# Overflow branch moved behind expert 13, the turn of expert 1 one unit later, the last projection piece reordered

## The chip, the cores and the metric

The kernel runs on one core of a Trainium2 chip. Its time is the device time of one execution in microseconds (us). A core has TensorE (PE, with PEld for its weight loads), VectorE (DVE), ScalarE (ACT), GpSimd (POOL) and SyncE (SP), each with its own queue of instructions that it works off in order, and 16 DMA engines that move data between the chip's memory and the core's.

## The reference

An encoder of two layers on 512 tokens of 1024 numbers, all in fp32. Each layer is an attention part and a mixture of experts:

```python
h = rms_norm(x, norm1_g[layer])
proj = jnp.einsum('bsd,dc->bsc', h, w_in[layer])          # cut into the inputs of four mixers
y_a = mla_mixer(...); y_b = dilated_mixer(...); y_c = gqa_mixer(...); y_d = diff_mixer(...)
mixed = jnp.concatenate([rms_norm(y_a), rms_norm(y_b), rms_norm(y_c), y_d], axis=-1) * mix_beta[layer]
x = x + jnp.einsum('bsm,md->bsd', mixed, w_out[layer])
x = x + hier_moe(rms_norm(x, norm2_g[layer]), ...)
# hier_moe: router picks one of 4 groups, then 2 of its 4 experts for each token; then
for e in range(N_EXPERTS):                                # 16
    hid = jax.nn.silu(t @ w_gate[e]) * (t @ w_up[e])      # 1024 -> 512
    y = y + gate[:, e:e + 1] * (hid @ w_down[e])          # 512 -> 1024
```

## The kernel before

**Products.** Weights come as fp32. ACT rounds a block of 128x1024 to `hi` (L155), DVE, in some places POOL, computes the rest `lo` (L156), and PE makes each product in three passes, hi by xh, lo by xh, hi by xl (`mm3`, L299). Expert 0 alone is multiplied in plain fp32 (L1504).

**Weights.** The class `Weights` (L158) holds all weights of the program in one list, in the order of their use, as units of 512 KB. SP issues their loads in that order, each as soon as a raw buffer comes free; a raw buffer comes free when its unit is split. Six pairs of hi and lo may be ahead of their use. In the expert stretch there are some 29 raw buffers, a few of them parts of the tile `x_sb` that the stretch does not need.

**Order.** The program is written under a manual schedule: each engine's instructions stand in its queue in the order in which the Python code issues them.

**Projection.** `stage` (L667) makes one piece of the in-projection for the four tiles of 128 tokens: `proj` issues the products of a tile, `W.split` the split of one more weight unit, `F.pump` some steps of a filler (here the norm of a mixer's queries and keys: a square on ACT, L451, and its sum on DVE, L455), and `ev()` the evacuation of the product by ACT (L763). The piece that begins at column 2208 is the last. Behind it come 64 attention units, each with a maximum over the scores on DVE (L936) and the exponent on ACT (L955); weights of the out-projection are split in between.

**Experts.** Each expert takes the tokens that chose it, up to 96, by a list. POOL gathers them from memory (`gather`), PE transposes them (`turn`, L1492), ACT and DVE split the transposed tokens into `xh` and `xl`. The matrices follow each other as `MOE_ORDER` says: (0, g), (0, u), (1, g), (0, d), (1, u), (2, g), (1, d), (2, u), ... (14, g), (13, d), (14, u), (15, g), (14, d), (15, u), (15, d), where g is gate, u up and d down, each of four units. After g comes the SiLU on ACT (`silu`, L1511), after d the weighting on ACT (`store`, L1546) and a scatter-add into memory by POOL.

**Overflow.** If an expert has more than 96 tokens, `overflow` (L1550) runs further rounds over all experts. It is a branch (L1562) on a number that every engine reads from the chip's memory; with these inputs the number is 1 and nothing of the body runs. The queues go through the branch one by one: what stands behind it on an engine is issued when that engine has passed it. In the kernel before it stands behind the store of expert 0, with the SiLU of expert 1 after it.

Of the kernel before, what the change touches and what calls it, by code (L numbers as in the profile page):

```python
# [21 lines left out]
NT = 4  # L22
EPS = 1e-6
NE = 16
# [39 lines left out]
def hybrid_encoder(ctx: ExitStack, tc: tile.TileContext, I: dict, out: bass.AP, depth=2, dbg=None):  # L64
# [183 lines left out]
    W = Weights()  # L248
# [105 lines left out]
    for layer in range(depth):  # L354
# [6 lines left out]
        X = {}  # L361
# [25 lines left out]
        with ExitStack() as c2:  # L387
# [203 lines left out]
            with ExitStack() as c3:  # L591
# [37 lines left out]
                def turned(t):  # L629
                    for k in range(0, 8, 4):  # L630
                        pt = turn([hs[t][:, (k + j) * 128:(k + j + 1) * 128] for j in range(4)])
                        split(hTh[t][:, k:k + 4], hTl[t][:, k:k + 4], pt.rearrange("p (a b) -> p a b", b=128))
# [21 lines left out]
                def proj(c0, t, evac, mid=None):  # L654
                    us, per, n = wbase[layer, 'in', c0]
                    pm = ps.tile([128, 512], FT, name="pm", tag="mm")[:, :n]
                    for i, u in enumerate(us):
                        wh, wl = W.get(u)
                        if mid and i == 2:
                            mid()  # L660
                        mm3(pm, [(hTh[t][:, k], hTl[t][:, k]) for k in range(i * per, (i + 1) * per)],
                            [(wh[:, j], wl[:, j]) for j in range(per)], first=i == 0, last=i == len(us) - 1)
                    if t == NT - 1:
                        W.free(us[-1] + 1)
                    return lambda: evac(t, pm)

                def stage(c0, evac, budget, then={}):  # L667

                    us = wbase[layer, 'in', c0][0]
                    for t in range(NT):  # L670
                        ev = proj(c0, t, evac)
                        for _ in side:
                            break
                        W.split(W.done + 1)
                        F.pump(budget)
                        if t == NT - 1:
                            W.split(us[-1] + 1 + 4)
                        ev()
                        if t in then:
                            then[t]()  # L680

# [79 lines left out]
                def copy_to(dst):  # L761
                    def ev(t, pm):
                        A.activation(dst[:, t], pm, AF.Copy, scale=rs[t])  # L763
                    return ev
# [15 lines left out]
                if layer == 0:  # L780
# [6 lines left out]
                    ev = proj(0, 1, ev_a, lambda: turned(2))  # L787
# [6 lines left out]
                    ev = proj(0, 2, ev_a, lambda: turned(3))  # L794
# [4 lines left out]
                for t in range(NT if layer else 0):  # L799
# [12 lines left out]
                    if t == 1:  # L812
                        ev = proj(0, 0, ev_a)
# [4 lines left out]
                    if t == 2:  # L818
                        ev = proj(0, 1, ev_a)
                        turned(2)  # L820
                    if t == 3:
# [4 lines left out]
                        ev = proj(0, 2, ev_a)  # L826
# [4 lines left out]
                ev = proj(0, 3, ev_a)  # L831
# [20 lines left out]
                od = O[3] = outputs(3, 256, 32, "pc", ap_)  # L852
# [1 line left out]
                assert lat['normed']  # L854
                stage(1696, copy_to(od[0]), 4, {0: lambda: prepare(heads[0], 0), 1: lambda: prepare(heads[0], 1)})
                F.add(norm(od, gains['diff_qk_g'], 32))
                stage(2208, copy_to(od[3]), 1)
                for _ in side:
                    pass
                del TP['hp']  # L860
# [2 lines left out]
            with ExitStack() as c3:  # L863
# [431 lines left out]
                g, d = list(range(32, 48)), list(range(48, 56))  # L1295
# [6 lines left out]
                for k, hd in enumerate(heads):  # L1302
                    first, m = place[k * NT], len(hd[2])
# [79 lines left out]
        with ExitStack() as c2:  # L1383
# [221 lines left out]
            def start(e):  # L1605
# [3 lines left out]
                else:  # L1609
# [5 lines left out]
                          m=lambda: G.memset(xg[1], 0.0), S=lambda: start(1), K=weights,  # L1615
                          q=lambda: G.tensor_copy(parts[..., :2], tokb[:, :, None].to_broadcast([128, NT, NE, 2])))
            tail(TAIL[len(seq) + 5])
            for e, m in MOE_ORDER:
                us = wbase[layer, e, m][0]
                for i, u in enumerate(us):  # L1620
                    W.split(u + 1)
                    end = e == NE - 1 and m != 'g'
                    if m == 'd':
                        X[e].down(i, W.get(u))
                    elif end:
                        X[e].half(i, W.get(u))
                    else:
                        X[e].gu(m, i, W.get(u))
                    W.free(u + 1)
                    if end:  # L1630
                        if m == 'u' and i % 2:
                            X[e].hidden(i // 2)
                        if (m, i) == ('u', 2) or (m, i) == ('d', 0):
                            X[e].turn_hidden(m == 'd')
                    elif m == 'g' and i == 0 and e > 0:
                        X[e - 1].hidden()
                    upto = moe_units[-1] + 1
                    if end and m == 'd' and i > 1:
                        upto += W.RAW
                    W.split(min(u + (AHEAD if end else W.HL), upto), G if (m, i) in GS and not end else V)  # L1640
                    if m == 'g' and i == TH and e > 0:
                        X[e - 1].turn_hidden()
                    if m == 'u' and i == 1 and e + 1 < NE:
                        X[e + 1].turn()

                    for s, todo in FIRST if e < 2 else ((e + 3, (('u', 0), ('u', 2))),):
                        if e > 1:
                            todo = [(e,) + w for w in todo]
                        if (e, m, i) in todo and s < NE:
                            (start if (e, m, i) == todo[1] else listed)(s)  # L1650
                    if m == 'd' and e < 2:
                        if i == 0:
                            X[e].hots = hots(e, sm.tile([128, NT, CAP], BF, name="oh", bufs=2))
                        elif i == 2:
                            X[e].lists(lambda t: parts[:, t, e], rows=e == 0)
                    if m == 'g' and i == 0 and e == NE - 1 and not last:
                        (place, g1), = W.room(1)
                        g1 = g1.bitcast(FT)
                        SP.dma_start(g1, _bcast(I['norm1_g'][layer + 1]))
                    if m == 'u' and i == 0 and e == NE - 1 and not last:  # L1660

                        pt = ps.tile([128, NT, 128], FT, name="pto", tag="tr")
                        for t in range(NT):
                            PE.matmul(pt[:CAP, t], X[e].hots[t], identb, start=True, stop=True)
                        place = place[:, :512].rearrange("p (t c) -> p t c", t=NT)
                        A.activation(place[:CAP], pt[:CAP], AF.Copy)
                        V.tensor_copy(wlast, gate[:, :, NE - 1])
                if m == 'g' and e != 1:
                    X[e].silu()
                elif m == 'd' and (last or e < NE - 1):  # L1670
                    X[e].store()
                if (e, m) == (0, 'd'):

                    overflow()
                    X[1].silu()
                if m == 'd' and e == NE - 2 and not last:

                    for t in range(NT):
                        SP.dma_start(x_sb[:, t], stream[:, t])
# [91 lines left out]
```

## Time and profile before

| | us |
|---|---|
| median of three runs | 1387.91 (1387.12 to 1390.14) |
| the profiled execution | 1392.77 |
| its span | 1391.0 |
| PE busy | 1290.2 (93% of the span) |
| DVE busy | 1057.1 (76%) |
| ACT busy | 857.8 (62%) |
| POOL busy | 359.9 (26%) |

The mean granted clock of TensorE over the span is 0.971. The program moves 278.44 MB, 200 GB/s on average. The two expert stretches are those in which the page's DMA row stands at nine tenths: roughly from 380 to 670 us and from 1060 to 1350 us. An idle time of an engine stands in brackets behind the instruction that ended it, with the engine or the transfer that released it.

### The profile page before, as it was taken

To read this page: it belongs to the slowest core of one execution; us is meant where nothing else is said; L and a number is where in the kernel's file an instruction comes from. 1 tells how busy PE (TensorE), PEld (TensorE's weight loads), DVE (VectorE), ACT (ScalarE), POOL (GpSimd) and SP (SyncE) were. 2 spreads that over 40 slices of the span, in tenths; PEclk is the share of its full clock that TensorE was granted. 3 is DMA by queue.
4 is the path that set the end of the run, shared out by engine and by line. 5 is a ranking of instruction groups with operands and counts; after the bars stand their busy time and mean duration, and the time that the engine had idled before them with its cause. 6 is when DMAs were issued, how large, how long until landed. Compare 5 with 4: busy or idle time off the path is not lost. (4 is left out here: it accounts for less than half of the span.)

```text
span 1391.0 us, 21081 instructions
## 1 busy us (share of the span) xinstructions
PE 1290.2 (93%) x7182; PEld 1003.5 (72%) x7182; DVE 1057.1 (76%) x2073; ACT 857.8 (62%) x1419; POOL 359.9 (26%) x580
## 2 busy tenths in 40 slices
PE   9998899999986999999989998999998699999996
PEld 7776688888844666666778886888885366676674
DVE  5537866878575999999776587586966499999994
ACT  5343366664245888888744545676634378888884
POOL 3105333324411411111041161430344132111120
PEclk9999899999998999999999999999999899999998
DMA  8322341024597999999344223211176899999950
GB/s 230 100 78 63 133 138 41 15 67 168 217 382 264 352 366 362 366 365 329 109 118 125 78 75 79 69 37 31 48 307 239 303 312 358 370 365 366 367 201 13
DMA packets 100575, 278.44 MB, mean 200 GB/s; under 512 B 19466, under 2 KB 30522, under 8 KB 100457
## 3 DMA queue, kind: packets, MB, share of 16 engines
q1 hardware_dynamic: 89816, 249.00, 49.9%
q0 software_dynamic: 10352, 27.41, 7.9%
q8 instruction: 58, 0.95, 0.3%
q10 hardware_dynamic: 288, 0.59, 0.1%
q14 instruction: 61, 0.49, 0.1%
HBM read 264.34 MB, written 24.81 MB: 208 GB/s over the span
## 5 line engine op out<-in xcount | busy, mean ns | idle before, releaser
L156 DVE TENSOR_TENSOR lo<-raw,hi 128x1024 fp32r<-128x1024 f32 (+2 forms) x387 | 463.9, 1221 | 64.2 <-ACT hi L155 56.1
L155 ACT ACTIVATE hi<-raw 128x1024 fp32r<-128x1024 f32 (+1 forms) x393 | 405.4, 1051 | 99.6 <-PE pg L299 28.7
L299 PE MATMUL pm<-lo,hTh 128*128 128x512 f32 (+2 forms) x376 | 132.5, 352 | 5.9 <-DVE lo L156 5.9
L299 PE MATMUL pm<-hi,hTh 128*128 128x512 f32 (+2 forms) x376 | 134.3, 357 | 0.7 <-ACT hTh L155 0.5
L299 PE MATMUL pm<-hi,hTl 128*128 128x512 f32 (+2 forms) x376 | 132.0, 351 | 0.2
L299 PE MATMUL pd<-hi,hl 128*96 128x512 f32 x256 | 102.5, 400 | 4.5 <-DVE hl L156 2.8
L986 PE MATMUL pv<-v,pT 128*128 128x64 f32 x768 | 99.0, 272 | 6.5 <-DVE pT L974 2.7
L299 PE MATMUL pd<-lo,hh 128*96 128x512 f32 x256 | 101.2, 395 | 1.6 <-DVE lo L156 1.6
L986 PEld LDWEIGHTS pv<-v,pT 128*128 128x128 f32 x768 | 94.3, 193 | 10.8 <-DVE pT L974 5.0
L299 PE MATMUL pu<-hi,xh 128*96 128x512 f32 (+1 forms) x256 | 101.1, 395 | 0.6 <-PEq L1562 0.6
L299 PE MATMUL pd<-hi,hh 128*96 128x512 f32 x256 | 101.2, 395 | 0.0
L957 ACT ACTIVATE p<-p,m 128x512 f32<-128x512 f32 x96 | 68.7, 716 | 52.1 <-DVE m L939 51.7
L299 PE MATMUL pu<-hi,xl 128*96 128x512 f32 (+1 forms) x256 | 98.2, 384 | 0.0
L299 PE MATMUL pu<-lo,xh 128*96 128x512 f32 (+1 forms) x256 | 98.2, 384 | 0.0
L299 PE MATMUL pg<-hi,xh 128*96 128x512 f32 x240 | 96.8, 404 | 0.0
L299 PE MATMUL pg<-lo,xh 128*96 128x512 f32 x240 | 95.6, 398 | 0.0
L299 PE MATMUL pg<-hi,xl 128*96 128x512 f32 x240 | 95.3, 397 | 0.0
L299 PEld LDWEIGHTS pm<-lo,hTh 128*128 128x128 f32 x376 | 71.0, 189 | 16.0 <-DVE lo L156 8.0
L299 PEld LDWEIGHTS pm<-hi,hTh 128*128 128x128 f32 x376 | 70.9, 188 | 12.0 <-ACT hTh L155 1.0
L299 PEld LDWEIGHTS pm<-hi,hTl 128*128 128x128 f32 x376 | 71.0, 189 | 9.5 <-DVE hTl L156 0.9
L307 PE MATMUL ptr<-ident,p 128*128 128x128 f32 x512 | 77.3, 273 | 0.3 <-DVE pT L974 0.2
L307 PEld LDWEIGHTS ptr<-ident,p 128*128 128x128 f32 x512 | 63.8, 141 | 17.7 <-DVE pT L974 1.2
(389 smaller groups left out, 2772.5 us busy)
## 6 DMA issues: line engine op xcount, KB each, us to landing
raw<-in_expert_w_down_dram SPq DMA_DIRECT2D x118, 512.0 KB
raw<-in_expert_w_gate_dram SPq DMA_DIRECT2D x114, 512.0 KB
raw<-in_expert_w_up_dram SPq DMA_DIRECT2D x110, 512.0 KB
raw<-in_w_in_dram SPq DMA_DIRECT2D x32, 512.0 KB
raw<-in_w_out_dram SPq DMA_DIRECT2D x16, 512.0 KB
toep<-brep SPq DMA_DIRECT2D x16, 448.0 KB
x_sb<-in_expert_w_gate_dram SPq DMA_DIRECT2D x14, 512.0 KB
x_sb<-in_expert_w_up_dram SPq DMA_DIRECT2D x10, 512.0 KB
```

What stands on the lines that cost most here:

```text
L155: A.activation(hi, src, AF.Copy)
L156: E.tensor_tensor(lo, src, hi.bitcast(FT), op=OP.subtract)
L299: PE.matmul(pt, a, b, start=first and n == 0, stop=last and n == tot - 1)
L307: PE.transpose(pt[:c, i * 128:(i + 1) * 128], s, ident)
L957: A.activation(p, p, AF.Exp, bias=m, scale=-1.0, accum_out=s)
L986: PE.matmul(st['pv'][:, t], self.pT[:, k * 128:(k + 1) * 128], self.v(k), start=k == 0, stop=k == NT - 1)
```

## The change

Three edits. `stage` gets a flag for the last piece: there the evacuation comes first, then, for the first two tiles only, one split, then the filler, and the splits of up to four units at the end are left out. The turn of expert 1 stands after the third unit of expert 0's up matrix and no longer after the second. The overflow branch stands behind expert 13's store, and the SiLU that comes after it is expert 14's.

```diff
-                def stage(c0, evac, budget, then={}):
+                def stage(c0, evac, budget, then={}, final=False):
                     us = wbase[layer, 'in', c0][0]
                     for t in range(NT):
                         ev = proj(c0, t, evac)
                         for _ in side:
                             break
-                        W.split(W.done + 1)
+                        if final:
+                            ev()
+                        if not final or t < 2:
+                            W.split(W.done + 1)
                         F.pump(budget)
-                        if t == NT - 1:
-                            W.split(us[-1] + 1 + 4)
-                        ev()
+                        if not final:
+                            if t == NT - 1:
+                                W.split(us[-1] + 1 + 4)
+                            ev()
...
-                stage(2208, copy_to(od[3]), 1)
+                stage(2208, copy_to(od[3]), 1, final=True)
...
-                    if m == 'u' and i == 1 and e + 1 < NE:
+                    if m == 'u' and i == (1 if e else 2) and e + 1 < NE:
                         X[e + 1].turn()
...
-                if m == 'g' and e != 1:
+                if m == 'g' and e != NE - 2:
                     X[e].silu()
                 elif m == 'd' and (last or e < NE - 1):
                     X[e].store()
-                if (e, m) == (0, 'd'):
+                if (e, m) == (NE - 3, 'd'):
                     overflow()
-                    X[1].silu()
+                    X[NE - 2].silu()
```

In the changed kernel the lines behind `stage` stand five further down (the branch is L1567 there, the SiLU L1516, the store L1551, the turn L1497, the evacuation L768).

ACT's queue in layer 0, at the old place of the branch, before. `ye` is the store of expert 0, `sg` the SiLU of expert 1, `xh` the tokens of expert 2; the branch's body is left out:

```order
L155 ACTIVATE hi<-x_sb 128x1024
L1546 ACTIVATE ye<-pd,w 96x512 x2
L1553 TENSOR_LOAD nrd
L1562 COMPARE_AND_BRANCH
...
L1562 UNCONDITIONAL_BRANCH
L1511 ACTIVATE sg<-pg 96x512
L155 ACTIVATE hi<-x_sb 128x1024
L155 ACTIVATE hi<-raw 128x1024
L155 ACTIVATE xh<-ptg 128x384 x2
```

The same place in the changed kernel:

```order
L155 ACTIVATE hi<-raw 128x1024
L1516 ACTIVATE sg<-pg 96x512
L155 ACTIVATE hi<-raw 128x1024 x3
L155 ACTIVATE hi<-x_sb 128x1024
L1551 ACTIVATE ye<-pd,w 96x512 x2
L155 ACTIVATE hi<-x_sb 128x1024
L155 ACTIVATE hi<-raw 128x1024
L155 ACTIVATE xh<-ptg 128x384 x2
```

The SiLU of expert 1 has moved up to the end of its gate, and between the store and the next splits nothing stands any more. The new place in the changed kernel, ACT's queue behind the store of expert 13, where `sg` is the SiLU of expert 14 and `xh` the tokens of expert 15:

```order
L155 ACTIVATE hi<-raw 128x1024 x5
L1551 ACTIVATE ye<-pd,w 96x512 x2
L1558 TENSOR_LOAD nrd
L1567 COMPARE_AND_BRANCH
...
L1567 UNCONDITIONAL_BRANCH
L1516 ACTIVATE sg<-pg 96x512
L155 ACTIVATE hi<-raw 128x1024 x2
L155 ACTIVATE xh<-ptg 128x384 x2
L155 ACTIVATE hi<-raw 128x1024 x5
```

Here two splits and the tokens of the last expert stand behind the branch. On SP all loads of a layer's expert weights now stand ahead of the branch, where before all but those of the first experts stood behind it.

PE's queue at the turn of expert 1 in layer 0, before (`pu` is expert 0's up product, `pli` the list of expert 0):

```order
L1504 MATMUL pu<-raw,xh 96x512 x4
L1492 MATMUL ptg<-ident,xg 128x96 x8
L1504 MATMUL pu<-raw,xh 96x512 x4
L1465 LDWEIGHTS oh
L1465 MATMUL pli<-parts,oh 96x5
```

And now:

```order
L1509 MATMUL pu<-raw,xh 96x512 x6
L1497 MATMUL ptg<-ident,xg 128x96 x8
L1509 MATMUL pu<-raw,xh 96x512 x2
L1470 LDWEIGHTS oh
L1470 MATMUL pli<-parts,oh 96x5
```

Two products, one unit, have moved ahead of the transposes. ACT's queue in the last projection piece of layer 0, before, up to the first attention unit's exponent (`h` is the filler's square, `v` the evacuation):

```order
L451 ACTIVATE h<-qk_1151 128x512
L763 ACTIVATE v_1152<-pm,r0y 128x256
L155 ACTIVATE hi<-raw 128x1024
L451 ACTIVATE h<-qk_1151 128x512
L763 ACTIVATE v_1152<-pm,r1y 128x256
L451 ACTIVATE h<-qk_1151 128x512
L763 ACTIVATE v_1152<-pm,r1y 128x256
L155 ACTIVATE hi<-raw 128x1024
L451 ACTIVATE h<-qk_1151 128x512
L763 ACTIVATE v_1152<-pm,r1y 128x256
L955 ACTIVATE p,den<-sc,m 128x512
```

And now:

```order
L768 ACTIVATE v_1152<-pm,r0y 128x256
L155 ACTIVATE hi<-raw 128x1024
L451 ACTIVATE h<-qk_1151 128x512
L768 ACTIVATE v_1152<-pm,r1y 128x256
L155 ACTIVATE hi<-raw 128x1024
L451 ACTIVATE h<-qk_1151 128x512
L768 ACTIVATE v_1152<-pm,r1y 128x256
L451 ACTIVATE h<-qk_1151 128x512
L768 ACTIVATE v_1152<-pm,r1y 128x256
L451 ACTIVATE h<-qk_1151 128x512
L960 ACTIVATE p,den<-sc,m 128x512
```

Each evacuation has moved ahead of a square, and between the third square and the exponent no split stands any more. The split that is missing here stands among the attention units, with its lo half on POOL.

## Rows read from the trace of the kernel before

**Rows 1.** Windows: start:end, length, busy PE, PEld, DVE, ACT, POOL, clock, DMA share, GB/s

```profile
446.00:660.00 214.00, 211.87 (x1031) 148.12 (x1030) 198.59 (x266) 176.48 (x211) 42.46 (x23) 1.00 1.01 358
660.00:664.00 4.00, 4.00 (x22) 2.87 (x21) 3.36 (x5) 3.35 (x6) 0.00 (x0) 1.00 0.44 181
1342.00:1346.00 4.00, 4.00 (x19) 2.81 (x18) 3.37 (x4) 3.85 (x5) 0.00 (x0) 1.00 0.18 75
424.00:446.00 22.00, 13.41 (x55) 9.47 (x56) 14.30 (x25) 13.04 (x16) 1.28 (x1) 0.77 0.63 203
1100.00:1124.00 24.00, 12.02 (x45) 8.02 (x44) 11.46 (x19) 10.00 (x13) 1.25 (x1) 0.72 0.62 194
```

**Rows 2.** Timeline, PE behind the branch: start, length, instruction, idle before and releaser

```profile
416.25 0.45 PE L299 MATMUL pu<-hi,xh 128*96 128x512 f32 x1 [0.30 <-PEq L1562]
...
432.59 0.78 PE L1465 MATMUL pli<-parts,oh 128*96 128x5 bf16 x4 [11.30 <-DVE oh L372]
...
1112.74 0.78 PE L1465 MATMUL pli<-parts,oh 128*96 128x5 bf16 x4 [11.98 <-DVE oh L372]
```

**Rows 3.** Timeline, ACT's first instruction behind the branch, layer 0

```profile
429.56 0.59 ACT L1511 ACTIVATE sg<-pg 96x512 f32<-96x512 f32 x1 [12.19 <-SPq L1562]
```

**Rows 4.** Timeline, SP's loads across the branch, layer 0

```profile
417.19 15.54 SPq L195 DMA_DIRECT2D x_sb<-in_expert_w_down_dram  x2
```

**Rows 5.** Windows behind the branch's stall, layers 0 and 1

```profile
432.00:438.00 6.00, 5.41 (x18) 3.79 (x19) 5.96 (x14) 3.87 (x7) 0.70 (x1) 0.60 0.63 181
1112.00:1120.00 8.00, 7.25 (x21) 4.94 (x22) 7.65 (x16) 4.96 (x7) 1.25 (x1) 0.54 0.68 202
```

**Rows 6.** Timeline, PE at the turn of expert 1, both layers

```profile
388.95 3.60 PE L1504 MATMUL pu<-raw,xh 128*96 128x512 f32 x8
396.49 1.51 PE L1492 MATMUL ptg<-ident,xg 96*128 96x96 f32 x8 [3.94 <-DMA xg<-h2d,nrd]
...
1076.24 1.51 PE L1492 MATMUL ptg<-ident,xg 96*128 96x96 f32 x8 [4.58 <-DMA xg<-h2d,nrd]
```

**Rows 7.** Windows behind the turn, layers 0 and 1

```profile
396.00:404.00 8.00, 7.51 (x21) 3.69 (x22) 1.85 (x7) 0.98 (x2) 0.00 (x0) 0.59 1.03 419
1076.00:1084.00 8.00, 7.76 (x23) 3.95 (x24) 2.31 (x10) 0.98 (x2) 0.00 (x0) 0.63 1.03 418
```

**Rows 8.** Timeline, ACT at the end of the last projection piece, layer 0

```profile
156.18 0.63 ACT L451 ACTIVATE h<-qk 128x512 f32<-128x512 f32 x1 [9.56 <-DVE ssq L455]
...
158.26 1.06 ACT L155 ACTIVATE hi<-raw 128x1024 fp32r<-128x1024 f32 x1 [1.09 <-DMA raw<-in_w_out_dram]
...
159.75 0.46 ACT L763 ACTIVATE v<-pm,r1y 128x256 f32<-128x256 f32 x1
```

**Rows 9.** Timeline, PE at the same place

```profile
157.23 1.09 PE L307 MATMUL ptr<-ident,qm 128*96 128x128 f32 x4 [5.68 <-ACT v L763]
```

**Rows 10.** Timeline, ACT, the store of expert 13, both layers

```profile
667.19 1.24 ACT L1546 ACTIVATE ye<-pd,w 96x512 f32<-96x512 f32 x2
...
1348.48 1.24 ACT L1546 ACTIVATE ye<-pd,w 96x512 f32<-96x512 f32 x2
```

**Rows 11.** Timeline, DVE, the tokens of expert 15, layer 1

```profile
1352.98 1.01 DVE L156 TENSOR_TENSOR xl<-ptg,xh 128x384 fp32r<-128x384 f32 x2
```

**Rows 12.** Timeline, PE, the first product of expert 15's gate, layer 1

```profile
1354.92 0.39 PE L299 MATMUL pg<-hi,xh 128*96 128x512 f32 x1
```

**Rows 13.** Timeline, DVE at the end of the last projection piece, layer 0

```profile
157.80 0.67 DVE L455 TENSOR_REDUCE ssq<-h 128x16 f32<-128x512 f32 x1
...
161.09 0.68 DVE L936 TENSOR_REDUCE m<-sc 128x1 f32<-128x512 f32 x1
```

**Rows 14.** Groups by line, POOL: count, busy us, mean ns, idle before

```profile
L156 POOL TENSOR_TENSOR lo<-raw,hi 128x1024 fp32r<-128x1024 f32 x6 | 14.2, 2365 | 10.4 <-ACT hi L155 10.4
```

**Rows 15.** Timeline, SP's loads of up matrices, layer 0

```profile
583.76 5.10 SPq L198 DMA_DIRECT2D raw<-in_expert_w_up_dram  x4
...
641.25 10.87 SPq L198 DMA_DIRECT2D raw<-in_expert_w_up_dram  x8
```

## The prediction

> **What bounds the kernel now.** I read the table of 40 slices first (PE at nine tenths or more in the expert stretches, DMA at nine there and low elsewhere), then the waits of PE and ACT, then timelines around each place that the change touches, then windows for clock and traffic. In the body of an expert loop both limits lie close together: from 446 to 660 us PE works 211.87 of 214 us at full clock, and DMA is at share 1.01 with 358 GB/s [rows 1]. So PE sets the time there as long as the weights, which arrive almost as slowly as they are used, keep their lead. Time is lost at three kinds of places, and the change touches each, in both layers.
>
> The first is the overflow branch behind expert 0. PE loses 0.30 us at its own branch, computes on for 5 us, and stands 11.30 us in layer 0; in layer 1 it stands 11.98 us [rows 2]. ACT stood 12.19 us at the branch [rows 3], and SP, which issues the weights, issued nothing between a load that began at 417.19 and ended 15.54 us later, so that the weights stop too [rows 4]. PE comes back at half clock: 0.60 on average from 432 to 438 and 0.54 from 1112 to 1120 [rows 5].
>
> The second is the turn of expert 1's gathered tokens: PE waits 3.94 and 4.58 us for the gather [rows 6], and works at reduced clock behind it, 0.59 and 0.63 over eight microseconds [rows 7]. The third is the end of the last projection piece: ACT stands 9.56 us behind a DVE reduction with an evacuation queued behind the blocked instruction [rows 8], and PE in layer 0 5.68 us for that evacuation [rows 9].
>
> **The branch leaves its old place.** PE gets back 0.30 + 11.30 and 0.30 + 11.98 = 23.88 us. The slow clock: 6 x (1 - 0.60) = 2.4 less about 0.3 for the 0.59 us in which PE was idle anyway gives 2.1; 8 x (1 - 0.54) = 3.7 less about 0.4 for 0.75 idle gives 3.3 [rows 5]. Sum 29.3 us. What could be late next there is the weights. Their stream also lost time: 22 x (1 - 0.63/1.01) = 8.3 us of traffic between 424 and 446, 24 x (1 - 0.62/1.01) = 9.3 in layer 1 [rows 1]. It gets these back; PE gets back more, so the lead of the weights shrinks, which costs nothing until the end of the stream has to be awaited. It is, at the new place.
>
> **The branch arrives behind expert 13.** I take the wait to be one for the transfers issued ahead of the branch: ACT's idle ends with SP's queue there [rows 3], and 12.19 us at 358 GB/s are 4.4 MB, eight loads of 0.52 MB, which is a full queue and no fixed price. At the new place all weights of the layer are issued ahead of it, so it waits for the last of them. Before, the stream of layer 0 ended at 660 + 4 x 0.44/1.01 = 661.7, that of layer 1 at 1342 + 4 x 0.18/1.01 = 1342.7 [rows 1]; less the 8.3 and 9.3 won back, 653.5 and 1333.4. ACT came to the end of expert 13's store at 667.19 + 1.24 and 1348.48 + 1.24 [rows 10]; it now comes 13.7 + 3.3 (the turn, below) = 17.0 us and 15.6 + 3.2 = 18.8 us earlier, plus 0.6 for the branch's own instructions (ACT's idle at the old place was that much longer than PE's, 12.19 to 11.60): 652.0 and 1331.5. The wait is the difference, 1.5 and 1.9 us, and ACT's stop with the 0.6 is 2.1 and 2.5.
>
> Behind it in ACT's queue stand the SiLU of expert 14, two weight splits and the xh of expert 15; PE's cover is the four units of expert 14's up projection. The margin before was small: xl of expert 15 was ready at 1352.98 + 1.01 = 1353.99 [rows 11], and PE began that expert's gate at 1354.92 [rows 12], needing xl two products later, at 1355.4: 1.4 us. The SiLU of 0.59 us [rows 3] now stands in that queue too, so I take the whole stop as PE's: 2.1 + 2.5, and 1 us each for the clock (the stall of 11 us cost 2.1 and 3.3, one of 4 us 3, above and below; a short one can cost none): minus 6.6. Bounds: the margin covers all but PE's own 0.30 twice, minus 0.6; or the stream is later than worked out, minus 20.6 in all (rival two).
>
> How fast the stream can be, two rows tell differently: 419 and 418 GB/s in the windows at 396 and 1076 us [rows 7], but 358 over the body of the loop, where scatter-adds and gathers run beside the loads [rows 1]; at 358 an expert's 6.29 MB take 17.6 us. The Trainium skill, page "DMA: Bandwidth & Descriptors", section "Bandwidth" with its table "Measured", gives 425 GB/s for 16 MB on a core that streams alone; by it an expert would be an estimated 14.8 us, the stream would be well ahead at the new place, and the 6.6 would be 0.6. The trace agrees with the page in those windows and not over the body, and the branch waits for the body.
>
> **The turn one unit later.** Two up units of expert 0 took 3.60 us [rows 6], so one takes 1.80, and it now runs while the gather is in flight: 3.94 becomes 2.14, 4.58 becomes 2.78, minus 1.80 each. What is then late: behind the transposes one unit of 1.80 us is left in place of two, ahead of expert 1's gate; half of xl's 1.01 us [rows 11], with about as much for xh, is 1 us and fits beside it (if it did not, the gate would start up to 1 us late). The slow clock behind the wait cost 8 x 0.41 = 3.3 less 0.25 idle = 3.05 and 8 x 0.37 = 3.0 less 0.1 = 2.85 [rows 7]; a wait half as long may keep the clock or lose it as before. I take half: 1.5 and 1.4. Sum 3.3 + 3.2 = 6.5, from 3.6 (clock no better) to 9.5.
>
> **The last projection piece.** The evacuation now stands ahead of the split and of the filler's square, and the third split is not in the piece at all. The blocked square and its 9.56 us remain. Behind it came an evacuation, a hi split (1.06 us, after 1.09 of wait for its load), the last square and the last evacuation at 159.75 [rows 8]; now the last evacuation comes right behind the blocked square, at about 156.7, and the last square at 157.2. From there DVE decides: it reduced the blocked square from 157.80, 0.67 us, would reduce the last one right behind it, and so begin the first maximum of the attention units at 157.80 + 2 x 0.67 = 159.1 in place of 161.09 [rows 13], since the lo half of the split is gone from its queue as well. That is 2.0 us, and I take the same for layer 1. Against this, one split a layer moves into the attention units: 1.06 us of ACT and 2.36 us of POOL (the six splits there took 2365 ns [rows 14]), both with idle time; I charge 0.5 in all. Sum 4.0 - 0.5 = 3.5. Bounds: if DVE's backlog alone decides, 0.5; at most 4.5.
>
> **Sum.** 29.3 + 6.5 + 3.5 - 6.6 = 32.7 us. The profiled execution took 1392.77 us (span 1391.0), so 1360.1 for it; it was 4.86 above the median of 1387.91, so the median comes to 1355.2, forecast 1355.
>
> **Rivals.** One: the stream has headroom. It is no longer interrupted, and in windows without gathers it ran at 419 GB/s [rows 7]; then there is no wait at the new place and 6.6 becomes 0.6: gain 38.7, 1349 us. The skill's figure quoted above speaks for it. Against it: share 1.01 through the whole body [rows 1], so that DMA had nothing to spare.
>
> Two: the stream ends later than by subtraction. Between the loads of the up matrices of experts three apart lie 641.25 - 583.76 = 57.49 us, 19.2 an expert [rows 15], which is more than the 17.6 of the weights alone. Were it 0.6 us an expert slower still over the 12 experts between the two places, 7 us are added in each layer: gain 18.7, 1369 us.
>
> Three: the branch's wait is a fixed 12 us wherever it stands, for instance SP's own reaction, and not a matter of weights. Then the new place costs 12.5 and the clock 2.7 in each layer, about what the old one did, and only 6.5 + 3.5 less about 1 remain: gain 9, 1379 us. For it: the waits were nearly alike in both layers (12.19 on ACT [rows 3], 11.30 and 11.98 on PE [rows 2]). Against it: SP issued nothing from the branch on [rows 4], so that the queue ran empty, which takes as long as there is something in it.
>
> Four: turn and piece yield nothing (the gather or DVE decides as before), the branch does as forecast: gain 22.7, 1365 us.
>
> Five, slower: the weights fall behind without the pause, and all at once at the branch. The other terms give 39.3, that is 19.6 us a layer; with 2.1 of that for clock and the branch itself, the stream must end 17.5 us later per layer than ACT arrives, 1.46 us an expert over 12 experts. On top of the 19.16 us of rival two the point is 20.6 us an expert; at 21.0 it is 22 us, 4.6 more a layer, and the time 1397 us. The measured pace falls short of it, and the pause that goes was no help to DMA in the first place [rows 1].
>
> **Numbers.** Forecast 0.57 (alone 1350 to 1361), headroom 0.17, later stream 0.13, fixed wait 0.05, turn and piece nothing 0.04, slower 0.04. The range 1345 to 1370 takes in the forecast, the first, second and fourth cases and leaves out the fixed wait and the slower one, and a tenth for what I did not see. About 0.2% (2.8 us) is what a measurement tells from no change: faster 0.94, within it 0.02 (a fixed wait with neither of the small gains), slower 0.04.
>
> **What would show it.** Right: no PE idle at the old place and full clock there; ACT stopped 2 to 3 us ahead of expert 14's SiLU in both layers, ended by weight transfers; PE's wait for the gather at about 2.1 and 2.8 us; the first maximum of the units 2 us earlier relative to the start of the piece. Wrong: a stop at the new place of 9 us or more (rival two if the last weight lands with it, rival three if it landed long before), or none at all (rival one); PE waiting for a split in the middle of the loop would make the prediction wrong altogether.

## The result, and the profile after

The changed kernel takes 1368.47 us (median of 4 runs, 1363.87 to 1369.35), the kernel before beside it 1388.89 us (1387.12 to 1390.14). The ratio is 0.9847 with a 95% interval of 0.9821 to 0.9873: faster by 20.4 us. The forecast was 1355 us in a range of 1345 to 1370; the time lies near the upper end of the range. The profiled execution took 1367.83 us with a span of 1365.9, so that the two profiled executions differ by 24.9 us, where 32.7 were forecast.

At the old place nothing is left of the stop. Windows of the changed kernel over the stretches that answer to the last two of [rows 1] (columns as there):

```profile
416.00:440.00 24.00, 23.26 (x121) 16.40 (x120) 22.74 (x41) 19.34 (x25) 2.93 (x3) 1.00 1.03 374
1086.00:1110.00 24.00, 23.21 (x118) 16.32 (x117) 22.74 (x39) 19.11 (x22) 3.75 (x3) 1.00 1.03 373
```

PE works 23.2 of 24 us at full clock, and DMA is at share 1.03 without a gap.

At the new place ACT's timeline shows the store of expert 13 and, behind the branch, the SiLU of expert 14, in both layers; they answer to [rows 3] and [rows 10]:

```profile
650.66 1.24 ACT L1551 ACTIVATE ye<-pd,w 96x512 f32<-96x512 f32 x2
658.73 0.59 ACT L1516 ACTIVATE sg<-pg 96x512 f32<-96x512 f32 x1 [6.83 <-SPq L1567]
...
1319.33 1.24 ACT L1551 ACTIVATE ye<-pd,w 96x512 f32<-96x512 f32 x2
1324.32 0.59 ACT L1516 ACTIVATE sg<-pg 96x512 f32<-96x512 f32 x1 [3.75 <-SPq L1567]
```

ACT is done with the store at 651.9, where the forecast had it at 652.0 with the branch's own 0.6 in it; but it stops for 6.83 and 3.75 us, not 2.1 and 2.5. PE's timeline a little later, at expert 15's gate, as in [rows 12]:

```profile
661.64 0.74 PE L299 MATMUL pg<-hi,xh 128*96 128x512 f32 x1 [4.02 <-ACT xh L155]
...
663.18 0.74 PE L299 MATMUL pg<-hi,xl 128*96 128x512 f32 x1 [0.37 <-DVE xl L156]
...
1327.23 0.47 PE L299 MATMUL pg<-hi,xh 128*96 128x512 f32 x1 [0.93 <-ACT xh L155]
...
1328.77 0.47 PE L299 MATMUL pg<-hi,xl 128*96 128x512 f32 x1 [0.84 <-DVE xl L156]
```

The stop reaches PE as a wait for xh and xl. Behind it the granted clock is at half, in layer 0 from 660.4 to 667.2 us (0.74 us a product in place of 0.39) and in layer 1 from 1329.4 to 1332.8. When did the weights end? Windows of DMA at the end of layer 0's stream, first the changed kernel, then the kernel before:

```profile
656.00:658.00 2.00, 1.62 (x7) 0.81 (x5) 0.00 (x0) 0.00 (x0) 0.00 (x0) 1.00 0.40 92
658.00:660.00 2.00, 0.00 (x0) 0.00 (x0) 0.00 (x0) 1.27 (x2) 0.00 (x0) 1.00 0.09 20
```

```profile
660.00:662.00 2.00, 2.00 (x13) 1.50 (x12) 1.79 (x3) 1.35 (x3) 0.00 (x0) 1.00 0.72 295
662.00:664.00 2.00, 2.00 (x11) 1.37 (x10) 1.56 (x2) 2.00 (x4) 0.00 (x0) 1.00 0.17 68
```

Both end in a tail: the share, a mean over the 16 engines, sinks from about 1 to 0 over some 4 us, and the last load has landed only at the end of it (the 0.09 behind 658 us is no weight any more). In the kernel before the last load of layer 0 landed at 663.9 and that of layer 1 at 1345.0, in the changed kernel at 658.0 and 1324.0. SP itself stands at the branch until then. It waits there for eight semaphores in each layer; the first of these waits ends at 658.0 in layer 0, the last at 1324.2 in layer 1:

```profile
L1567 SPq EVENT_SEMAPHORE  x16: 17/17/17, 658.0 to 1324.2; - x16
```

At the turn of expert 1, PE in both layers, as in [rows 6]:

```profile
398.22 0.85 PE L1497 MATMUL ptg<-ident,xg 96*128 96x96 f32 x8 [2.44 <-DMA xg<-h2d,nrd]
...
1067.02 0.82 PE L1497 MATMUL ptg<-ident,xg 96*128 96x96 f32 x8
```

The wait is 2.44 us (2.14 forecast) and none (2.78 forecast), and the transposes run at full clock. The end of the last projection piece in layer 0, ACT and PE, as in [rows 8, 9]:

```profile
157.22 0.63 ACT L451 ACTIVATE h<-qk 128x512 f32<-128x512 f32 x1 [7.59 <-DVE ssq L455]
157.76 0.46 ACT L768 ACTIVATE v<-pm,r1y 128x256 f32<-128x256 f32 x1
```

```profile
152.38 0.60 PE L307 MATMUL ptr<-ident,qm 128*96 128x128 f32 x4
...
158.27 1.15 PE L317 MATMUL pw<-tri 128*128 128x256 bf16 x6 [4.59 <-ACT v L768]
```

The blocked square is still there, and PE waits now at filler products that need the same evacuation. DVE begins the first maximum at 160.22 in place of 161.09 [rows 13]:

```profile
160.22 0.68 DVE L941 TENSOR_REDUCE m<-sc 128x1 f32<-128x512 f32 x1
```

Counted from the start of the piece's last product it comes after 8.66 us in place of 10.53, and in layer 1 after 5.51 in place of 7.40: 1.9 us earlier in both.

Holding the start of one PE product in one trace against the same product in the other gives what had been won up to each point (us):

| up to | before | after | won so far | this part | forecast |
|---|---|---|---|---|---|
| layer 0, out-projection | 355.06 | 356.57 | -1.5 | piece -1.5 | +1.75 |
| layer 0, behind the turn | 402.78 | 399.77 | 3.0 | turn +4.5 | +3.3 |
| layer 0, behind the old place | 442.64 | 426.46 | 16.2 | +13.2 | +13.7 |
| layer 0, behind the new place | 675.74 | 666.28 | 9.5 | -6.7 | -3.1 |
| layer 1, expert 0's gate | 1062.49 | 1056.25 | 6.2 | piece -3.2 | +1.75 |
| layer 1, behind the turn | 1081.82 | 1068.11 | 13.7 | turn +7.5 | +3.2 |
| layer 1, behind the old place | 1123.96 | 1095.25 | 28.7 | +15.0 | +15.6 |
| layer 1, behind the new place | 1357.69 | 1332.65 | 25.0 | -3.7 | -3.5 |

Two terms fail: the piece loses 4.7 us where 3.5 were to be won, and the new place costs 10.4 in place of 6.6. The turn seems to win twice what was forecast.

The rows hold all that happened between two products, and not the piece or the turn alone. In layer 1, 3.0 of the 3.2 us in the row "piece" were lost at half clock between 1049.5 and 1056.3 us, at expert 0's gate and just ahead of it. The gate in the kernel before and in the changed one:

```profile
1061.20 7.03 PE L1504 MATMUL pg<-raw,xh 128*96 128x512 f32 x16
```

```profile
1053.69 8.34 PE L1509 MATMUL pg<-raw,xh 128*96 128x512 f32 x16
```

PE came that much later to the gather and did not wait for it, so that the same 3 us come back in the 7.5 of the turn. In layer 0, 1.0 of the 1.5 us was lost by 125 us, ahead of the piece. Against this some 3 us were won behind the attention units, where the kernel before ran at half clock (351.4 to 354.8 and 1030.7 to 1034.1 us) and the changed one did not. So -4.7 is no measure of the piece; the experiments give one.

### The profile page after: what moved, and what is told of

Its sections match the earlier page's. It is cut to its first block, busy times and chain, and to the rows that moved or that the text cites. A ratio compares the mean times of both kernels' runs of the same rounds, so it can differ in the third digit from the quotient of the medians.

```text
span 1365.9 us, 21099 instructions
## 1 busy us (share of the span) xinstructions
PE 1288.9 (94%) x7182; PEld 1005.9 (74%) x7182; DVE 1055.0 (77%) x2071; ACT 858.2 (63%) x1419; POOL 343.5 (25%) x582
## 5 line engine op out<-in xcount | busy, mean ns | idle before, releaser
L991 PEld LDWEIGHTS pv<-v,pT 128*128 128x128 f32 x768 | 94.5, 194 | 10.5 <-DVE pT L979 4.5
L307 PE MATMUL ptr<-ident,p 128*128 128x128 f32 x512 | 80.1, 281 | 0.3 <-DVE pT L979 0.2
```

What stands on the lines that cost most here:

```text
L307: PE.transpose(pt[:c, i * 128:(i + 1) * 128], s, ident)
L991: PE.matmul(st['pv'][:, t], self.pT[:, k * 128:(k + 1) * 128], self.v(k), start=k == 0, stop=k == NT - 1)
```

## The experiments

Times are medians; "before" is the kernel before on the same chip.

**Single edits.** What is each edit worth alone?

```diff
# e1, the branch alone (with the SiLU that goes with it); e7 has this and the next
-                if (e, m) == (0, 'd'):
+                if (e, m) == (NE - 3, 'd'):
# e2, the turn alone
-                    if m == 'u' and i == 1 and e + 1 < NE:
+                    if m == 'u' and i == (1 if e else 2) and e + 1 < NE:
# e3, the piece alone
-                stage(2208, copy_to(od[3]), 1)
+                stage(2208, copy_to(od[3]), 1, final=True)
```

Branch alone: 

> The kernel before with the branch alone moved behind expert 13. By the two traces laid side by side the old place gave back 28.2 us and the new one cost 10.4, so the first theory (the trace of one execution tells what each edit is worth) expects a gain of 18 us, 1371 us, with ACT stopped 5 to 9 us in layer 0 and 3 to 6 us in layer 1 behind expert 13's store. The rival, that the three edits do not add up, since the turn's gain shifts PE against the weights and lengthens the wait at the new place, expects a shorter stop here (the turn gave PE 4.5 and 7.5 us, so a stop shorter by about as much, 1 to 3 us) and a gain of 22 us or more.

Measured 1363.95 against 1389.95 us, ratio 0.9814 (0.9791 to 0.9837): 26.0 us. ACT's stops there, layer 0 and layer 1:

```profile
654.07 0.59 ACT L1511 ACTIVATE sg<-pg 96x512 f32<-96x512 f32 x1 [3.39 <-SPq L1562]
...
1321.36 0.59 ACT L1511 ACTIVATE sg<-pg 96x512 f32<-96x512 f32 x1 [4.90 <-SPq L1562]
```

The gain is the rival's; the stop of layer 0 is shorter than the first theory had it, that of layer 1 is as it had it. The branch alone does better than the whole change.

Turn alone: 

> The kernel before with the turn of expert 1 alone moved one unit later. The first theory, from the two traces, expects 4.5 us in layer 0 and up to 7.5 in layer 1, a gain of 9 to 12 us. The prediction's sum gave 6.5. The rival, that PE's time won here is given back at the overflow branch right behind it, since PE then waits for the same transfers, expects 0 to 3 us: the stall at the old place grows from 11.3 and 12.0 us by what the turn wins.

Measured 1390.16 us, ratio 1.0003 (0.9986 to 1.0019): nothing. ACT at the branch behind expert 0, both layers:

```profile
428.59 0.59 ACT L1511 ACTIVATE sg<-pg 96x512 f32<-96x512 f32 x1 [16.59 <-SPq L1562]
...
1108.70 0.59 ACT L1511 ACTIVATE sg<-pg 96x512 f32<-96x512 f32 x1 [17.47 <-SPq L1562]
```

In layer 0 ACT goes on at nearly the moment of [rows 3], 428.59 to 429.56, but the stop is 16.59 in place of 12.19 us: what PE won at the turn (it was up to 5.4 us ahead of the kernel before) it waited out at the branch, and kept 1 us. The rival holds.

Piece alone: 

> The kernel before with the last projection piece alone reordered. The first theory expects a loss of 2 to 5 us: the first attention units run at half clock for longer, 15 us in layer 0 in place of 7, though their first maximum comes about 2 us earlier against the piece's start. The rival, that the clock there differs from one execution to the next in either kernel, expects a difference within 1.5 us of none, or a gain of up to 3.5 as the prediction had it.

Measured 1394.6 us, ratio 1.0029 (1.0014 to 1.0043): 4.65 us slower, as the first theory said.

Branch and turn: 

> Branch and turn moved, the piece as before. The first theory, by which the piece loses 4.7 us, expects a gain of 25 to 30 us against the kernel before, 4 to 5 us better than the whole change. The rival, that the piece is worth nothing or 3.5 us, expects 17 to 20 us, the whole change or a little slower.

Measured 1364.24 against 1389.95 us, ratio 0.9826 (0.98 to 0.9852): 25.7 us, the first theory. The turn adds nothing to the branch's 26.0, and the single edits add up: 26.0 - 0.2 - 4.65 = 21.1, the whole 20.4.

**Where the branch stands.** Turn moved, piece as before, branch behind expert 14 (e5), behind expert 12 (e6), or nowhere (e4):

```diff
-                if (e, m) == (NE - 3, 'd'):
+                if (e, m) == (14, 'd'):        # e5; in e6 (12, 'd'), in e4 nowhere
                     overflow()
-                    X[NE - 2].silu()
+                    X[15].silu()               # e5; in e6 X[13]
```

> The turn moved, the piece as before, the branch behind expert 12's store, 18 us earlier than behind expert 13's. First theory, the branch waits for every load that stands ahead of it on SP, and by then nearly all loads of the layer do: the wait ends at nearly the same moment as behind expert 13, so ACT stops for 18 to 24 us and the time is 1364 + 2 x 16 = 1396 us, slower than the kernel before. Rival, the wait is for a full queue of eight loads wherever the branch stands: ACT stops for about 12 us as behind expert 0, and the time is 1376 us.

Measured 1401.03 us, ratio 1.0071 (1.0049 to 1.0092): slower than the kernel before. ACT's stops:

```profile
653.89 0.59 ACT L1511 ACTIVATE sg<-pg 96x512 f32<-96x512 f32 x1 [22.60 <-SPq L1562]
...
1341.18 0.59 ACT L1511 ACTIVATE sg<-pg 96x512 f32<-96x512 f32 x1 [23.36 <-SPq L1562]
```

22.6 and 23.4 us, in the first theory's 18 to 24; eight loads, 12 us, are ruled out. With the same turn and piece and the branch behind expert 13 (e7) the two stops are 4.46 and 5.50 us:

```profile
652.05 0.59 ACT L1511 ACTIVATE sg<-pg 96x512 f32<-96x512 f32 x1 [4.46 <-PE pu L299]
...
1319.28 0.59 ACT L1511 ACTIVATE sg<-pg 96x512 f32<-96x512 f32 x1 [5.50 <-SPq L1562]
```

(The profile names a product of PE at the first; SP's last semaphore came at 651.90 there.) The last weight of layer 0 landed at 653.2 us, ACT went on at 653.9; with the branch alone behind expert 13 the two moments were 653.4 and 654.1, with the whole change 658.0 and 658.7. The wait ends with the last load that stands ahead of the branch on SP. It is so in all 16 stops of the eight kernels with the branch behind expert 0, 12 or 13: ACT goes on 0.2 to 0.7 us behind the landing of that load, and 0.13 to 0.16 us behind the last semaphore that SP waits for.

> The turn moved, the piece as before, the branch behind expert 14's store, with expert 15's SiLU after it. First theory: the branch waits for the last weight that was issued ahead of it, and that has landed by then, since expert 14's store comes 18 us after expert 13's: ACT stops for 0.5 to 1.5 us, and the time is that without a branch plus 1 to 3 us, 1355 to 1358. Rival, a price of the branch by itself: ACT stops again for 3 to 7 us and the time stays at 1364.

Measured 1352.28 us (1351.7 to 1353.56), ratio 0.9727 (0.9704 to 0.9751), 37.4 us faster than before and the fastest kernel of this study. ACT's first instruction behind the branch:

```profile
666.61 0.59 ACT L1511 ACTIVATE sg<-pg 96x512 f32<-96x512 f32 x1 [0.67 <-DVE wlast L1667]
...
1330.48 0.59 ACT L1511 ACTIVATE sg<-pg 96x512 f32<-96x512 f32 x1 [2.48 <-PE pu L299]
```

ACT stands for 0.67 and 2.48 us, and SP does not end either stop; the layer's last weights had landed at 651.9 and 1314.4. In layer 0 the first loads of the next layer stand ahead of the branch as well. The last of them landed at 662.6, 3.3 us before ACT came. The time lies 3 us below what the first theory expected.

> The turn moved, the piece as before, and the overflow branch left out altogether (the rounds for experts with more than 96 tokens, which do not run with these inputs, are missing). First theory: the branch behind expert 13 costs what the trace of the kernel with the same turn and piece shows there, 4.4 us in layer 0 and 6.6 in layer 1, so the time falls from 1364.2 by 9 to 11 us to 1354. Rival: without the stop the weights are late for the last two experts and PE waits for splits in its place; then 1360 to 1364.

Measured 1356.47 us, but from 1346.61 to 1360.17, ratio 0.9751 (0.971 to 0.9791): within its spread the same as with the branch behind expert 14. The theory's 1354 lies inside, and a branch that waits for no load costs nothing that these runs could tell.

**What the turn is worth without a wait behind it.** e5 with the turn as before:

> The branch behind expert 14, turn and piece as in the kernel before, to be held against 1352.3 with the turn moved. First theory: the turn wins 6 us a layer where it stands, and it was worth nothing with the branch behind expert 0 or 13 only because the branch's wait ended at a time set by the transfers; behind expert 14 it waits for nothing, so without the turn the kernel is 8 to 12 us slower, 1360 to 1364. Rival: the weights are as late either way and take the gain back somewhere else: 1352 to 1355.

Measured 1357.2 us, ratio 0.9764 (0.9745 to 0.9784), against 1352.28: 4.9 us, between the two. (The 1352.28 is from another chip; the kernel before took 1389.63 us there and 1389.86 here.) So the turn does win, once nothing waits for transfers behind it, but less than the first theory had it. That theory's figure came from the trace of before, where PE ran expert 0's gate at full clock and then waited 3.94 and 4.58 us [rows 6]. In this experiment PE waited less at the same place:

```profile
395.35 0.85 PE L1492 MATMUL ptg<-ident,xg 96*128 96x96 f32 x8 [0.90 <-DMA xg<-h2d,nrd]
...
1057.91 0.85 PE L1492 MATMUL ptg<-ident,xg 96*128 96x96 f32 x8 [1.13 <-DMA xg<-h2d,nrd]
```

It had run expert 0's 16 gate products in 8.42 and 8.29 us in place of 7.03, came later to a gather that was no later, and kept its clock behind it. Which of the two happens differs between executions of kernels that do not differ ahead of that place (from 380 to 388 us the granted clock was 1.00 in the kernel before and 0.71 in the one with the branch alone), so that one trace is a poor price for it.

**The piece.** First theory: the order lets PE start early and then wait, and the half clock that follows eats the gain. In the whole change I filled the wait with products:

```diff
-                        warm(WARM[2])
+                        warm(*((45, "tr") if i == 1 else (WARM[2],)))   # 45 fillers, in a buffer free at once
```

> The whole change, and in PE's wait for the last evacuation of the last piece 45 filler products (128x256, bf16, about 0.11 us each) in place of 6, in a buffer that does not wait for that evacuation. First theory: the piece loses its gain and more to the half clock of the first attention units; with PE busy through the wait the clock stays up, the units start about 2 us earlier than before, and the time falls from 1368.5 by 5 to 8 us. Rival: the clock is not the cause, the units are paced by DVE and ACT: the time stays within 2 us of 1368.5, or gets longer by the fillers that outlast the wait.

Measured 1367.62 us, ratio 0.9853 (0.9824 to 0.9883): the rival. Windows at the first attention units, the changed kernel and then this one:

```profile
160.00:170.00 10.00, 8.88 (x34) 7.28 (x33) 6.46 (x16) 4.67 (x11) 0.00 (x0) 0.50 0.51 193
170.00:180.00 10.00, 10.00 (x58) 9.04 (x57) 6.89 (x15) 4.61 (x10) 1.46 (x2) 0.72 0.71 264
180.00:190.00 10.00, 10.00 (x80) 9.30 (x79) 7.58 (x14) 5.76 (x13) 2.59 (x4) 1.00 0.39 93
```

```profile
160.00:170.00 10.00, 8.14 (x64) 7.25 (x63) 7.18 (x20) 5.13 (x13) 0.00 (x0) 1.00 0.50 200
170.00:180.00 10.00, 8.38 (x39) 7.17 (x38) 7.51 (x14) 4.30 (x11) 2.91 (x4) 0.69 0.77 261
180.00:190.00 10.00, 10.00 (x65) 9.18 (x64) 5.18 (x10) 5.31 (x13) 1.14 (x2) 0.80 0.29 70
```

The clock was full from 160 to 170 in place of half, and PE was 6.8 us ahead of the changed kernel at 168.8. Then it had to wait 1.6 us for DVE and the clock fell after all: it was at half from 173.8 to 184.1 us, in the changed kernel from 158.6 to 175.7. By 184 us 0.2 us of the lead was left. The half clock moved, the time did not.

So I took the piece's two halves apart, on the kernel with the branch behind expert 14 (1352.28 with the piece as before):

```diff
# e9, the order alone
+                        if final:
+                            ev()
                         W.split(W.done + 1)
...
-                        ev()
+                        if not final:
+                            ev()
# e10, the splits alone
-                        W.split(W.done + 1)
+                        if not final or t < 2:
+                            W.split(W.done + 1)
                         F.pump(budget)
-                        if t == NT - 1:
+                        if not final and t == NT - 1:
                             W.split(us[-1] + 1 + 4)
                         ev()
```

> The whole change with the branch behind expert 14 in place of 13, to be held against 1352.3 with the piece as before. First theory: the piece costs 4 us of PE time in the attention units, whatever stands behind, so 1356 (1354 to 1359). Rival: it cost only through the branch behind expert 13, where the weights came later with it: 1352.

Measured 1356.74 us, ratio 0.9754 (0.9729 to 0.9779): 4.5 us lost, as expected; the loss does not come through the branch.

> Branch behind expert 14, turn moved, and of the piece only the order: the evacuation first, then all splits as before. First theory: the order lets PE begin the first attention units early and then wait, after which the clock falls for longer; that costs the 4 us: 1356. Rival: the cost comes from the split that moved into the attention units: 1352.

Measured 1352.82 us, ratio 0.9725 (0.9702 to 0.9748): the order alone costs nothing, and wins nothing. It does not bring the first maximum forward either:

```profile
161.56 0.68 DVE L939 TENSOR_REDUCE m<-sc 128x1 f32<-128x512 f32 x1
```

That is 10.60 us behind the start of the piece's last product, as against 10.73 in e5, and in layer 1 7.65 against 7.45.

> Branch behind expert 14, turn moved, and of the piece only the splits: two in place of three and more, the evacuations in their old place behind the filler. First theory: 1352, since the order is what costs. Rival: 1356, since the late split on ACT and POOL is what costs.

Measured 1360.38 us, ratio 0.9783 (0.9761 to 0.9804): 8.1 us slower. The first theory falls; the late split is what costs. Taking the splits out of the piece is also what brings the first maximum forward: that comes after 8.62 and 5.51 us here, after 8.67 and 5.50 in the kernel with the whole piece (e12). And once the splits have moved, the order does count: 1360.38 us without it, 1356.74 with it. The place shows in POOL's and PE's timelines. POOL in the kernel with the order alone (e9), then POOL and PE in the one with fewer splits (e10):

```profile
199.53 0.73 POOL L524 TENSOR_TENSOR qst<-qk,qst 128x256 fp32r<-128x256 f32 x1 [4.83 <-ACT qst L521]
```

```profile
200.75 2.37 POOL L156 TENSOR_TENSOR lo<-raw,hi 128x1024 fp32r<-128x1024 f32 x1 [5.45 <-ACT hi L155]
203.08 0.72 POOL L524 TENSOR_TENSOR qst<-qk,qst 128x256 fp32r<-128x256 f32 x1
```

```profile
203.86 0.66 PE L307 MATMUL ptr<-ident,qst 128*128 128x128 f32 x4 [1.23 <-POOL qst L524]
```

The moved split's lo half, 2.37 us on POOL, stands directly ahead of the query product `qst`, which PE transposes next. The whole change has the same two lines in both layers on PE:

```profile
204.36 0.66 PE L307 MATMUL ptr<-ident,qst 128*128 128x128 f32 x4 [1.23 <-POOL qst L524]
...
216.76 1.12 PE L307 MATMUL ptr<-ident,kst 128*128 128x128 f32 x4 [1.59 <-POOL kst L538]
...
873.19 0.66 PE L307 MATMUL ptr<-ident,qst 128*128 128x128 f32 x4 [1.24 <-POOL qst L524]
...
885.60 1.11 PE L307 MATMUL ptr<-ident,kst 128*128 128x128 f32 x4 [1.60 <-POOL kst L538]
```

The wait at `qst` is new: it stands, with 1.22 to 1.24 us, in both layers of all five kernels with the late split, and at this place in none of the other nine. The wait of 1.6 us at `kst` is in every kernel. Behind it the clock fell to half in 7 of 10 cases with the late split and in 6 of 18 without it, one of them in layer 0 of the kernel before. So the fall is more frequent with the late split, but it is not shown to come from it. Against e5, the kernel with the whole piece (e12) loses 1.25 us at 202, about as much again behind 215, 1.5 at 864 and 1.3 behind 877: 5.3 us in all, of which about 1 came back at expert 0's gate in layer 0. In e10 some 3.8 us more went at half clock between 841.6 and 851.8 us in layer 1; one trace does not tell whether that belongs to the edit, but the medians of five executions each, 3.6 us apart between e10 and e12, speak for it.

## Why the prediction was right, and where it was not

**The branch leaves its old place.** 29.3 us forecast, 28.2 in the traces. Right, with the clock. The weights won back their traffic too: the last load of layer 0 landed 5.9 us earlier in the changed kernel and 10.5 earlier with the branch alone, where 8.3 were forecast.

**The wait is for the weights ahead of the branch.** Right, and shown by moving the branch both ways: one expert earlier the stop grew by 18.1 and 17.9 us (e6 against e7), one expert later no load was waited for. Rival three, a fixed wait, is excluded by that, rival five by the result. The row [rows 4] was read too simply: its 15.54 us span two loads, the second issued at 432.4, and SP was held between them by its semaphores at the branch, up to 429.4.

**The size of that wait.** This term was mis-sized: -6.6 forecast, -10.4 in the traces. The step that failed is "the stream of layer 0 ended at 660 + 4 x 0.44/1.01 = 661.7, that of layer 1 at 1342 + 4 x 0.18/1.01 = 1342.7". An average share tells how much was moved, not when the last engine was done; the last loads had landed at 663.9 and 1345.0, 2.2 and 2.3 us later. With these two landings the prediction's own sum gives stops of 4.3 and 4.8 us and -11.1 for the term; in the kernels with the branch behind expert 13 the stops were 3.4 to 6.8 us. In layer 0 of the changed kernel ACT's arrival came out within half a microsecond, but the last load landed 2.4 us later than the 663.9 less the 8.3 won back. The later start of the expert stretch (-1.5 in the table) would account for 1.5 of that; the rest stays open. Rival two named this side, with another cause. The 425 GB/s of the Trainium skill ("DMA: Bandwidth & Descriptors", "Bandwidth"), which spoke for rival one, was not reached: 374 GB/s from 416 to 440 us, and the stream was not ahead.

**The turn.** 6.5 forecast. The traces show 12.0 in the changed kernel, the runs 0 (alone and beside the branch) and 4.9 where the branch waits for nothing. The step's mechanism was right, the unit fills the wait for the gather. Of the 12.0, 3.0 are what layer 1 had lost at half clock just ahead. What failed is the addition in "29.3 + 6.5 + 3.5 - 6.6": the turn lets PE arrive earlier at a branch whose end is set by transfers, so its gain and the branch's cost may not be added. I moved ACT's arrival by the turn's 3.3 and 3.2 us and took that into the wait for the new place, which is why the sum did not come out much worse; but the loads landed later than I took them to, and by the runs nothing of the turn's gain outlived the stop.

**The piece.** +3.5 forecast, -4.65 in the runs (that the rows of the table add up to -4.7 is chance). Wrong in sign, and outside its bounds. Two steps failed. The first is "That is 2.0 us", taken as time of the kernel. The first maximum did begin 1.9 us earlier, in both layers. But by the late split PE was 1.5 us ahead in layer 1 alone; in layer 0 it had lost 0.5, with a half clock from 158.6 to 175.7 us in place of 153.5 to 163.7. The second is "both with idle time; I charge 0.5 in all": POOL was 26% busy over the span, and yet the 2.36 us landed directly ahead of a product that PE was about to need, in both layers. The waits at `qst`, 1.23 us each, make 2.5 of the loss; the rest shows as stretches at half clock, whose place differs between executions, and is not tied to the split. The price stood in the row of the six splits on POOL [rows 14]; what was not looked up is what comes behind them in POOL's queue.

**The sum.** 1368.5 less 1355.2 is 13.3 us. The terms came 7.6 short in the traces (32.7 less 25.1): 8.2 in the piece, 3.8 at the new place and 1.1 at the old one, against 5.5 more at the turn. The rest is the step "it was 4.86 above the median": the profiled execution of the changed kernel was 0.6 below its own median, and its distance from the median was taken as if it would stay. By the runs, medians against medians, the shares are others: 26.0 from the branch alone where 29.3 - 6.6 = 22.7 were forecast, -0.2 from the turn in place of 6.5, -4.65 from the piece in place of 3.5. Rival two's time, 1369, is the nearest of the list, but by luck: it puts 14 us more at the new place, where 3.8 more were lost. Rival four's 1365 is the next, and half of its mechanism holds: nothing from the turn, but a loss from the piece. The range held since the large term, the branch, was right; that two edits of three won nothing used up nearly all of the 15 us that it reached above the forecast, and that the time still lies 1.5 us inside is in part luck.

## What to carry to other kernels

The branch that every engine passes was here a barrier for all loads that SP had issued ahead of it: put such a branch where those have landed anyway (behind expert 14 the margin in layer 0 was 3.3 us), and don't add up gains that stand ahead of such a wait. What a moved instruction costs was decided here by its next neighbour in the queue and who waits for that one, not by its engine's idle share. The end of a stream is the landing of its last transfer, some 2 us behind where the mean share puts it here.

## What the runs showed of the hardware

With the branch one expert earlier the stop was 22.60 and 23.36 us, longer than behind expert 0 (12.19): it ended, as everywhere, 0.2 to 0.7 us behind the landing of the last load ahead of the branch on SP, whether or not PE needed that load next. And the half clock moved without moving the time: filling one wait of 4.6 us shifted it from 158.6 to 175.7 us to 173.8 to 184.1, and the kernel took 1367.6 us in place of 1368.5.
